# Head outputs stored by ScalarE or from the merge tensor, gates stored by GpSimd, v, q and k split some steps later

## The chip, the cores and the metric

The kernel runs on one core of a Trainium2 chip. A core has engines that work side by side, each through its own instructions in order: TensorE (PE in the profile; PEld is its weight load) multiplies matrices, VectorE (DVE) and ScalarE (ACT) work on elements, GpSimd (POOL) does small work and issues transfers, SyncE (SP) only issues transfers. Transfers (DMA) are issued from the queues of SP, ACT and POOL and are moved by 16 DMA engines. Engines wait for one another by semaphores. The metric is the device time of one execution in microseconds; lower is better.

## The reference

One block of a decoder: 512 rows of width 1024, all in float32. Cut to what matters:

```python
hn = rmsnorm(x, g_mix)
(xa, ba, ca, za, q, k, v, o, zb, ig, fg, ga, gb) = split(hn @ w_in)
ya = (ba * causal_short_conv(ca * xa, conv_w, conv_b) * silu(za)) @ w_a_out
hb = mlstm_chunkwise(q, k, v, ig + b, fg + b)          # 4 heads, dk 256, dv 512
yb = (sigmoid(o) * rmsnorm(hb, g_head) * silu(zb)) @ w_b_out
x  = x + (sigmoid(ga) * ya + sigmoid(gb) * yb) @ w_o
x  = x + sigmoid(rmsnorm(x, g_ple) @ w_ple_gate) * (p @ w_ple)
return rmsnorm(x, g_final)
```

Each head weighs the values v by decayed scores of q and k, divides by a sum, and is normalised and gated.

## The kernel before

**Products.** A float32 operand is split in two: hi, a rounded copy (ACT, L180 for weights), and lo, the rest (DVE, L181). Each product of two operands is three matmuls (L233, L234, L235: hi hi, hi lo, lo hi). Most large products go through `strassen`, which multiplies 2x2 blocks with seven products instead of eight. Product j has two steps of twelve matmuls each (i = 0, 1). Partial results stay in four PSUM banks (acc, bb, cc twice over i); between products ACT takes copies of them (`snap`, L346, tiles s and v) and DVE combines them (`out`, L350) into sums c, of which tag "c" has three buffers. A finished tile goes to a sink: `sink(n, t, src)` gets column half n and row tile t. Products 0 to 6 of a call hand over t2 (n = 0, t = 0 and 1) in steps 4 and 5, t5 and t6 (n = 1) in steps 9 to 13 and the last two tiles (n = 0, t = 2 and 3) straight from PSUM after step 12.

**Weights.** A chunk of weights is loaded by SP (L148) into one of four wraw buffers, split in two halves of 1024 columns, one per step, one product ahead of its use. Sums of chunks that the seven products need are made in place after a split, by an accumulating transfer on POOL's queue (L156, `add_chunk`: it adds a chunk from memory to the tile) or by DVE (L185).

**The order of work.** PE, ACT, DVE and POOL run in the order in which the code is written out. After each step the code calls `step`, and so `tick`: a tick first starts the sinks handed over at the step before, then splits one half of a weight chunk, then takes every running generator (`active`) one `yield` further. A `yield` more is therefore one step later, and what stands at the same tick is queued on each engine in that order. SP's transfers are ordered by the scheduler.

**Tiles.** A pool gives every tag a place (or several); a new tile of a tag waits until all that reads or writes the old one is done. In pool "heads" tag "vv" and tag "qk" have one place each. In turn tag "vv" holds: vv of a head (hi and lo of v), yc (16 KB per partition: blocks to be turned and their result), vv of the next head, and after the last head the tile ya1 of the convolution. Tag "qk" holds qk (hi and lo of q and k), then gty (the gates and the head's output y), then qk of the next head, at last ya0.

**A head** (`head(h, qk)`). A strassen call computes v and o (`sink_vo`): n = 0 tiles are v, split by ACT (L975) and DVE (L978); n = 1 tiles are o, which go through a sigmoid into gty (for odd heads times z, loaded back by POOL at L991). At the same time `scores` runs: score matmuls sc, exponentials on ACT (L916), products on DVE, split into pr. Then come the weighted sums (tile pv) and the normalisation. Even heads have two more strassen calls behind them: z of this head and the next (`sink_z`, stored to z_d by POOL at L1029) and the output gates of the merge (`sink_gate`, L781: a sigmoid, then a store to sg_d from ACT's queue, L782; eight stores a call). Head 2 begins with a call for q and k of heads 2 and 3 (`sink_qk`). The order is: head 0 with z and gates, head 1, head 2 with z and gates, head 3, the convolution (four strassen calls, `sink_conv`), the merge, the last products.

**Turning a head's output** (`turning`, `finish`). y has rows on partitions; the product with w_b_out needs columns there. DVE transposes 32x32 blocks (L810, `turn`), then 16 copies (`move`; ACT at L819, DVE at L817) put the blocks at their places in `spread`, and two transfers (`put`, L822, POOL's queue) store the halves to yt_d, which is loaded again long after. For even heads `finish` runs over the gate call: eight steps of copies, `put(0)`, two turns, six steps of copies, and `put(1)` at the third step of the next head's call. For heads 1 and 3 it runs over the next call and stores both halves at the end.

**q and k of odd heads** (`recut`) were stored to qk_d; during the gate call they are loaded at its eighth step by SP (L869) into a free part of yc and split into qk (L240, L241) three steps later, one of four parts each step.

**The merge tensor** m holds 4 row tiles of 1024 columns. It is allocated after the last head. During the convolution columns 512 and up of row tiles 2 and 3 serve as scratch (ct; L445, L447, L452); the first product of the merge (`gate_conv`, L1155) is the first to write the rest.

Of the kernel before, what the change touches and what calls it, by code (L numbers as in the profile page):

```python
# [20 lines left out]
NH = 4  # L21
# [15 lines left out]
def hybrid_block(ctx, tc, x, p, g_mix, w_in, conv_w, conv_b, w_a_out, b_gates, g_head,  # L37
                 w_b_out, w_o, g_ple, w_ple_gate, w_ple, g_final, out):
    nc = tc.nc
# [30 lines left out]
    H2 = S // 2  # L70
# [197 lines left out]
    yt_d = [dram.tile([P, 2, HC, H2], F32, name=f"yt_d{h}") for h in range(NH)]  # L268
    qk_d = {h: dram.tile([P, 4, S], F32, name=f"qk_d{h}") for h in (1, 3)}
    sg_d = [dram.tile([P, NT, CW], F32, name=f"sg_d{g}") for g in range(4)]  # L270
# [12 lines left out]
    def temp(tag, name=None, dt=F32):  # L283

        return tp.tile([P, S], dt, name=name or tag, tag=tag, bufs={"c": 3}.get(tag, 2))
# [492 lines left out]
    def sink_gate(g):  # L778
        def sink(n, t, src):
            sg = temp("e", "sg") if n == 0 and t > 1 else src  # L780
            act.activation(sg, src, AF.Sigmoid)  # L781
            nc.scalar.dma_start(sg_d[g + n][:, t, :], sg)  # L782
            yield
        return sink

# [10 lines left out]
        a = POFF[j] + (t - j) * P  # L796
        return u[:, a:a + P]

    def turning(h, half):

        both = hp.tile([P, 2, NT, DV], F32, name="yc", tag="vv", align_bytes=256)
        spare, blocks, spread = both[:, 0], both[:, 0], both[:, 1].rearrange("p t v -> p (t v)")
        n = NT
        if half:
            n = NT // 2
            blocks, spread = both[:, 1, :n], both[:, 1, n:].rearrange("p t v -> p (t v)")
        spread = spread.rearrange("p (v s) -> p v s", v=HC)

        def turn(y, t):
            dve.transpose(blocks[:, t % n, :], y[:, t, :])  # L810

        def move(i, on_dve):
            b, q = divmod(i, P // B)
            src = blocks[b * B:(b + 1) * B].rearrange("p t (v q a) -> p t v q a", q=P // B, a=B)[:, :, :, q]
            dst = spread[q * B:(q + 1) * B].rearrange("p v (t b a) -> p t v b a", t=n, a=B)[:, :, :, b]
            if on_dve:
                dve.tensor_copy(dst, src)  # L817
            else:
                act.activation(dst, src, AF.Copy)  # L819

        def put(i):
            nc.gpsimd.dma_start(yt_d[h][:, i], spread if half else spread[:, :, i * H2:(i + 1) * H2])  # L822

        return turn, move, put, spare

    def moves(move, plan):

        todo = deque(range((P // B) ** 2))
        for n_act, n_dve in plan:
            for i in range(max(n_act, n_dve)):  # L830
                if i < n_act:
                    move(todo.popleft(), False)
                if i < n_dve:
                    move(todo.popleft(), True)
            yield
        assert not todo

    def finish(h, y, tools):

        turn, move, put, _ = tools or turning(h, False)  # L840
        if h % 2 == 0:
            yield from moves(move, [(2, 0), (2, 0), (3, 0), (3, 0), (2, 0), (1, 0), (2, 0), (1, 0)])
            put(0)
            for t in (2, 3):
                turn(y, t)
                yield
            yield from moves(move, [(0, 1), (0, 1), (1, 3), (1, 1), (2, 2), (2, 2)])
            put(1)
            return
        for _ in range(4):  # L850
            yield
        for ts in ((0,), (1,), (2,), (3,)) if h == 1 else ((0, 1), (), (2,), (3,)):
            for t in ts:
                turn(y, t)
            yield
        yield from moves(move, [(1, 1)] * 8 if h == 1 else [(3, 0), (3, 1), (2, 1), (1, 1), (2, 2)])
        for i in range(2):
            put(i)

    def qk_tile():  # L860
        both = hp.tile([P, 2, 4, S], F32R, name="qk", tag="qk", align_bytes=256)
# [2 lines left out]
    def recut(h, raw, qk):  # L864

        for _ in range(7):
            yield
        for m in range(4):
            nc.sync.dma_start(raw[:, m, :], qk_d[h][:, m, :])  # L869
        yield  # L870
        yield
        yield
        qk.extend(qk_tile())
        for m in range(4):
            cut(qk[0][:, m, :], qk[1][:, m, :], raw[:, m, :])
            if m < 3:
                yield
# [69 lines left out]
    def head(h, qk):  # L947
        vv = []

        def sink_qk(n, t, src):  # L950

            fs, ps = slice(2 * (t % 2), 2 * (t % 2) + 2), slice(t // 2 * H2, (t // 2 + 1) * H2)
            src = src.rearrange("p (f s) -> p f s", f=2)
            if n == 1:
                nc.gpsimd.dma_start(qk_d[h + 1][:, fs, ps], src)
                return
            for _ in range(4 if t < 2 else 0):
                yield
            if not qk:
                qk.extend(qk_tile())  # L960
            cut(*[u[:, fs, ps] for u in qk], src)
            yield

        if h == 2:
            strassen(hn_lhs, sink_qk, True)
        pr = [hq2.tile([P, 1280], F32R, name=f"pr{i}", align_bytes=256) for i in range(2)]
        pp = hq2.tile([P, 1280], F32, name="pp")
        gt = []

        def sink_vo(n, t, src):  # L970
            if n == 0:
                if not vv:
                    both = hp.tile([P, 2, NT, DV], F32R, name="vv", tag="vv", align_bytes=256)
                    vv.extend(both[:, i] for i in range(2))
                act.activation(vv[0][:, t, :], src, AF.Copy)  # L975
                if t < 2:
                    yield
                dve.tensor_tensor(vv[1][:, t, :], src, vv[0][:, t, :].bitcast(F32), ALU.subtract)  # L978
            elif h % 2:
                so = temp("e", "so")  # L980
                act.activation(so, src, AF.Sigmoid)
                dve.tensor_tensor(gt[0][:, t, :], gt[0][:, t, :], so, ALU.mult)
            else:
                act.activation(gt[0][:, t, :], src, AF.Sigmoid)
            yield

        def scored():
            both = hp.tile([P, 2, NT, DV], F32, name="gty", tag="qk", align_bytes=256)
            gt.extend(both[:, i] for i in range(2))
            if h % 2:  # L990
                nc.gpsimd.dma_start(gt[0], z_d[h])  # L991

        active.append(scores(h, qk, pr, pp, scored))
        strassen(hn_lhs, sink_vo)
        gt, y = gt

        def weighted_sum(t, ps):
            dve.tensor_scalar(y[:, t, :], ps, inv[:, t:t + 1], None, ALU.mult)
            junk = temp("e", "junk")
            act.activation(junk, y[:, t, :], AF.Square, accum_out=hss[:, t:t + 1])  # L1000
            yield

        for t in range(NT):
            ps = ps_x.tile([P, S], F32, name="pv", tag="x")
            for j in range(t + 1):
                mm3(ps, [ptile(u, j, t) for u in pr], [u[:, j, :] for u in vv], j == 0, j == t)
            step(weighted_sum(t, ps))

        def norm(t):
            dve.scalar_tensor_tensor(y[:, t, :], y[:, t, :], hr[:, t:t + 1], gt[:, t, :], ALU.mult, ALU.mult)  # L1010

        def rsqrt():
            a, r, e = htmp
            dve.tensor_scalar(a, hss, 1.0 / DV, EPS, ALU.mult, ALU.add)
            pool.tensor_tensor(r, a, mhalf, ALU.pow)
            yield
            newton(e, a, r)
            dve.tensor_tensor(hr, r, e, ALU.mult)
            for t in range(NT) if h % 2 else ():
                norm(t)  # L1020
                if t == 1:
                    yield

        def sink_z(n, t, src):
            sz = temp("e", "sz")
            act.activation(sz, src, AF.Sigmoid)
            if n == 1:
                dve.tensor_tensor(src, sz, src, ALU.mult)
                nc.gpsimd.dma_start(z_d[h + 1][:, t, :], src)  # L1029
                yield  # L1030
                return
            dve.tensor_tensor(sz, sz, src, ALU.mult)
            dve.tensor_tensor(gt[:, t, :], gt[:, t, :], sz, ALU.mult)
            yield
            norm(t)
            yield
            if t < 2:
                yield
                if not tools:
                    tools.extend(turning(h, True))  # L1040
                tools[0](y, t)
                yield

        tools = []
        active.append(rsqrt())
        if h % 2 == 0:
            strassen(hn_lhs, sink_z)
        return y, tools
# [5 lines left out]
    for h in range(NH):  # L1054
        y, tools = head(h, qks[h])
# [9 lines left out]
    m = mp.tile([P, NT, D], F32, name="m", tag="m")  # L1065
# [216 lines left out]
    half = [slice(0, CW), slice(CW, D)]  # L1282
# [228 lines left out]
```

## Time and profile before

| | us |
|---|---|
| median of 3 runs | 863.88 (863.15 to 866.61) |
| the profiled execution | 864.66 |
| its span, first to last instruction | 862.8 |
| its mean granted TensorE clock | 0.989 |

The span leaves 1.9 us around it. In the profile a row of a group shows the line, engine and operation, out<-in by tile, how often, the busy time and the mean ns of one, and the idle time of the engine just before with what ended it. In the views of waits "A <- B: total, times, longest" says that A stood until B was done. Matmuls overlap, so their time is read from start to start.

### The profile page before, as it was taken

The numbers are of one execution on the slowest core, as the hardware profiler recorded it, in microseconds if no ns is written. First come the engines' busy times: TensorE is split into PE (matmuls) and PEld (weight loads), VectorE is DVE, ScalarE is ACT, GpSimd is POOL, SyncE is SP. The second block draws the span as 40 slices with busy tenths as digits, with TensorE's granted clock in tenths as the row PEclk, the third lists the DMA queues.
The fourth block names the chain that finished last, engine by engine and source line by source line (L and its number), as shares of the span: only waits on it lengthen the run. The fifth ranks groups of instructions, "written<-read, shape, count | busy, mean of one in ns | idle before, by whom it ended". The sixth has DMA issues, their size and how long they took to land.

```text
span 862.8 us, 12094 instructions
## 1 busy us (share of the span) xinstructions
PE 834.4 (97%) x4520; PEld 723.8 (84%) x4520; DVE 672.1 (78%) x927; ACT 528.6 (61%) x783; POOL 213.7 (25%) x207
## 2 busy tenths in 40 slices
PE   9999999999999989999989997999999999999996
PEld 7888888887789968888777996999998888888885
DVE  5787768995688747789758896888885688899665
ACT  6467655876755746667865583555555456567643
POOL 5203131103124411220212334242421122222031
PEclk9999999999999999999999998999999999999998
DMA  9749799679879987995988788898899668999502
GB/s 314 261 135 198 167 219 227 154 244 249 205 163 180 233 210 184 250 214 164 242 211 207 135 197 174 167 185 200 153 232 390 158 167 209 273 268 229 196 1 98
DMA packets 104515, 173.88 MB, mean 202 GB/s; under 512 B 5696, under 2 KB 46196, under 8 KB 103688
## 3 DMA queue, kind: packets, MB, share of 16 engines
q0 software_dynamic: 40064, 70.33, 43.9%
q1 hardware_dynamic: 59792, 94.64, 33.2%
q10 hardware_dynamic: 4600, 8.14, 3.1%
q8 instruction: 35, 0.57, 0.3%
q14 instruction: 24, 0.20, 0.1%
HBM read 156.30 MB, written 16.79 MB: 201 GB/s over the span
## 4 chain that ended last, share of the span: by engine, by line
PE 79%; DMA 6%; ACT 6%; DVE 4%; issue 3%; POOL 1%; ACTq 0%; SPq 0%; POOLq 0%; DVEq 0%
PE mm L235 24%; PE mm L234 24%; PE mm L233 24%; DMA yt_d<-yc 5%; ACT whi L180 2%; DVE wlo L181 2%; PE pv L234 1%; PE pv L233 1%; PE pv L235 1%; DMA gty<-z_d 1%; ACT yc L819 1%; DMA xin<-in_x 1%; POOL wraw L156 1%; ACT qk L240 1%; ACT c L781 0%
## 5 line engine op out<-in xcount | busy, mean ns | idle before, releaser
L181 DVE TENSOR_TENSOR wlo<-wraw,whi 128x1024 fp32r<-128x1024 f32 x244 | 299.2, 1227 | 109.2 <-ACT whi L180 103.5
L180 ACT ACTIVATE whi<-wraw 128x1024 fp32r<-128x1024 f32 x246 | 257.9, 1054 | 87.1 <-PE mm L235 34.4
L156 POOL DMA_DIRECT2D wraw<-in_w_in x112 | 137.5, 1410 | 342.3 <-DVE wlo L181 277.8
L233 PE MATMUL mm<-whi,hs 128*128 128x512 f32 x256 | 101.2, 395 | 8.2 <-ACT v L346 8.2
L234 PE MATMUL mm<-wlo,hs 128*128 128x512 f32 x256 | 101.2, 395 | 0.3 <-DVE wlo L181 0.3
L235 PE MATMUL mm<-whi,hs 128*128 128x512 f32 x256 | 101.1, 395 | 0.0
L346 ACT ACTIVATE s<-mm 128x512 f32<-128x512 f32 x84 | 50.2, 598 | 82.0 <-PE mm L235 80.5
L235 PE MATMUL mm<-hn_hi,wlo 128*128 128x256 f32 (+1 forms) x304 | 93.9, 309 | 6.5 <-DVE wlo L181 6.4
L233 PE MATMUL mm<-hn_hi,whi 128*128 128x256 f32 (+1 forms) x304 | 93.9, 309 | 0.0
L234 PE MATMUL mm<-hn_lo,whi 128*128 128x256 f32 (+1 forms) x304 | 93.4, 307 | 0.0
L235 PE MATMUL mm<-hs,wlo 128*128 128x256 f32 x320 | 90.6, 283 | 0.0
L233 PE MATMUL mm<-hs,whi 128*128 128x256 f32 x320 | 90.6, 283 | 0.0
L234 PE MATMUL mm<-hs,whi 128*128 128x256 f32 x320 | 90.6, 283 | 0.0
L234 PE MATMUL mm<-wlo,hn_hi 128*128 128x512 f32 x192 | 75.5, 393 | 3.6 <-DVE wlo L181 3.6
L233 PE MATMUL mm<-whi,hn_hi 128*128 128x512 f32 x192 | 74.9, 390 | 0.0
L235 PE MATMUL mm<-whi,hn_lo 128*128 128x512 f32 x192 | 74.8, 390 | 0.0
L235 PEld LDWEIGHTS mm<-hn_hi,wlo 128*128 128x128 f32 x304 | 58.7, 193 | 9.7 <-DVE wlo L181 6.9
L233 PEld LDWEIGHTS mm<-whi,hs 128*128 128x128 f32 x256 | 48.7, 190 | 18.7 <-ACT v L346 8.8
L234 PEld LDWEIGHTS mm<-hs,whi 128*128 128x128 f32 x320 | 61.5, 192 | 0.0
L233 PEld LDWEIGHTS mm<-hs,whi 128*128 128x128 f32 x320 | 61.5, 192 | 0.0
L235 PEld LDWEIGHTS mm<-hs,wlo 128*128 128x128 f32 x320 | 61.5, 192 | 0.0
L233 PEld LDWEIGHTS mm<-hn_hi,whi 128*128 128x128 f32 x304 | 58.8, 193 | 2.4
(340 smaller groups left out, 1726.3 us busy)
## 6 DMA issues: line engine op xcount, KB each, us to landing
wraw<-in_w_in SPq DMA_DIRECT2D x32, 1024.0 KB, 5.3
wraw<-in_w_in POOLq DMA_DIRECT2D x52, 512.0 KB, 7.9
wraw<-in_w_in SPq DMA_DIRECT2D x48, 512.0 KB, 4.9
wraw<-in_w_in POOLq DMA_DIRECT2D x60, 256.0 KB, 5.8
wraw<-in_w_b_out SPq DMA_DIRECT2D x7, 1024.0 KB, 6.4
wraw<-in_w_b_out POOLq DMA_DIRECT2D x12, 512.0 KB, 6.5
wraw<-in_w_o SPq DMA_DIRECT2D x5, 1024.0 KB, 7.9
yt_d<-yc POOLq DMA_DIRECT2D x8, 512.0 KB, 8.8
```

The lines of the kernel that those rows point to most:

```text
L156: nc.gpsimd.dma_start(raws[to][:, ks, cs], src[:, ks, :], accum_op=ALU.add)
L180: act.activation(hi, t, AF.Copy)
L181: (e_lo or dve).tensor_tensor(lo, t, hi.bitcast(F32), ALU.subtract)
L233: pe.matmul(ps, lhsT=a[0], rhs=b[0], start=first, stop=False, **kw)
L234: pe.matmul(ps, lhsT=a[0], rhs=b[1], start=False, stop=False, **kw)
L235: pe.matmul(ps, lhsT=a[1], rhs=b[0], start=False, stop=last, **kw)
L240: act.activation(hi, src, AF.Copy)
L346: act.activation(to[i], src, AF.Copy, scale=scale)
L819: act.activation(dst, src, AF.Copy)
```

## The change

1. The gates of the merge are stored from GpSimd's queue (sixteen stores).
2. The second half of the turned outputs of heads 0 and 2, and both halves of head 1, are stored from ScalarE's queue; the first half of heads 0 and 2 and both of head 3 stay with GpSimd.
3. For the last six steps of copies of even heads the plan (copies by ACT, by DVE) is another; ACT makes 4 instead of 6 and DVE 12 instead of 10.
4. The last head's copies put the blocks into row tiles 0 and 1 of m instead of the second half of yc, and the stores read m.
5. q and k of odd heads are split 2 steps later after their load.
6. In heads 1 to 3 the first two row tiles of v are split 4 steps later.

```diff
 def sink(n, t, src):
     sg = temp("e", "sg") if n == 0 and t > 1 else src
     act.activation(sg, src, AF.Sigmoid)
-    nc.scalar.dma_start(sg_d[g + n][:, t, :], sg)
+    nc.gpsimd.dma_start(sg_d[g + n][:, t, :], sg)
     yield
...
-def turning(h, half):
+def turning(h, half, place=None):
...
+    if place is not None:
+        spread = place.rearrange("p t v -> p (t v)")
     spread = spread.rearrange("p (v s) -> p v s", v=HC)
...
-    def put(i):
-        nc.gpsimd.dma_start(yt_d[h][:, i], spread if half else spread[:, :, i * H2:(i + 1) * H2])
+    def put(i, queue=nc.gpsimd):
+        queue.dma_start(yt_d[h][:, i], spread if half else spread[:, :, i * H2:(i + 1) * H2])
...
 def finish(h, y, tools):
-    turn, move, put, _ = tools or turning(h, False)
+    turn, move, put, _ = tools or turning(h, False, m[:, :2, :] if h == NH - 1 else None)
     if h % 2 == 0:
...
-        yield from moves(move, [(0, 1), (0, 1), (1, 3), (1, 1), (2, 2), (2, 2)])
-        put(1)
+        yield from moves(move, [(1, 2), (1, 2), (0, 2), (0, 2), (1, 2), (1, 2)])
+        put(1, nc.scalar)
         return
...
     for i in range(2):
-        put(i)
+        put(i, nc.scalar if h == 1 else nc.gpsimd)
...
 def recut(h, raw, qk):
...
-    yield
-    yield
-    yield
+    for _ in range(5):
+        yield
     qk.extend(qk_tile())
...
 def sink_vo(n, t, src):
     if n == 0:
+        for _ in range(4 if t < 2 and h else 0):
+            yield
         if not vv:
```

## What the change is predicted to do

> **What bounds the kernel now.** First the page: the span and the engines' busy time.
>
> ```profile
> span 862.8 us, 12094 instructions
> ...
> PE 834.4 (97%) x4520; PEld 723.8 (84%) x4520; DVE 672.1 (78%) x927; ACT 528.6 (61%) x783; POOL 213.7 (25%) x207
> ```
>
> TensorE (PE) is the bound at 97% busy. The change removes no matmul, so it can only close PE's idle time. The view of waits, for PE alone, names who ended that (total, times, longest):
>
> ```profile
> PE mm L233 <- ACT v L346: 8.2, 3, 3.9
> PE mm L235 <- DVE wlo L181: 6.4, 1, 6.4
> PE mm L234 <- DVE wlo L181: 3.9, 6, 0.9
> ```
>
> That is 18.5 us. The chain of waits (start, us, what) shows what stood behind the first two rows:
>
> ```profile
> 207.06 10.13 DMA yt_d<-yc
> 217.38 0.44 issue
> 217.81 0.59 ACT v L346
> 218.44 0.50 PE mm L233
> ...
> 300.47 11.76 DMA yt_d<-yc
> ...
> 433.46 10.15 DMA yt_d<-yc
> ...
> 520.03 7.52 DMA yt_d<-yc
> 527.57 0.69 DVE ya L410
> ```
>
> All four are one pattern. The store of a head's turned outputs still reads `yc`; the next tile of tag `vv` (vv at L975, ya at L410) has the same place; the in-order engine that first writes it stands, and behind it the splits and snapshots that PE needs. The gaps sum to 8.2 + 6.4 = 14.6 us: the three in the heads, the longest 3.9, and one in the convolution. The third, from PE's waits between 444 and 470 us, is
>
> ```profile
> PE mm L233 <- ACT v L346: 2.2, 1, 2.2
> ```
>
> so the first is 8.2 - 3.9 - 2.2 = 2.1 us. A gap can also cost clock afterwards. In the view by stretches of time the granted clock is the third number from the end of a row:
>
> ```profile
> 217.00:232.00 15.00, 13.55 (x55) 11.15 (x56) 10.98 (x17) 10.14 (x18) 3.01 (x3) 0.89 0.78 161
> ...
> 444.00:460.00 16.00, 14.82 (x67) 12.06 (x68) 13.03 (x20) 12.25 (x20) 2.99 (x3) 1.00 0.78 189
> ```
>
> ```profile
> 314.00:316.00 2.00, 2.00 (x7) 1.25 (x7) 1.57 (x2) 2.00 (x6) 0.00 (x0) 0.66 0.01 2
> 316.00:318.00 2.00, 2.00 (x5) 1.53 (x5) 1.24 (x3) 2.00 (x5) 0.00 (x0) 0.50 0.57 140
> ...
> 530.00:532.00 2.00, 1.95 (x9) 1.95 (x10) 1.93 (x4) 0.00 (x0) 0.00 (x0) 0.50 0.34 79
> 532.00:534.00 2.00, 2.00 (x15) 2.00 (x14) 1.93 (x5) 0.00 (x0) 1.26 (x2) 0.73 1.06 373
> ```
>
> Time lost is length times (1 - clock): 15 x 0.11 = 1.65 after the first gap, 0.68 + 1.00 after the second, nothing after the third, 1.00 + 0.54 after the fourth; 4.9 us. The four gaps are worth 14.6 + 4.9 = **19.5 us**: 11.6 in the heads (8.2 + 3.3), 7.9 in the convolution (6.4 + 1.5).
>
> [...]
>
> **The change part by part.** A step of the seven-product routine is twelve matmuls:
>
> ```profile
> 226.33 0.39 PE L233 MATMUL mm<-whi,hs 128*128 128x512 f32 x1
> ...
> 229.05 0.39 PE L233 MATMUL mm<-whi,hs 128*128 128x512 f32 x1
> ```
>
> That is 2.72 us; score matmuls lengthen some steps.
>
> *v split 4 steps later (heads 1 to 3).* The vv write leaves the queue in front of snapshot L346 and comes 4 x 2.72 = 10.9 us later. The longest hold was 3.9 us, so this part alone should clear the head gaps: **11.6 us**. It moves, per head, two ACT splits and two DVE subtractions; the weighted sums that need them stand at the end of the call, three steps or more behind. The sums c that they read are held longer: of the three buffers of c, each is rewritten one step after its late subtraction, by DVE itself, so DVE's own order covers it. One step less and DVE would stand for 2.7 us.
>
> *Turned outputs stored by ScalarE (second half of heads 0 and 2, both halves of head 1).* Four issues leave POOL's queue, where they stood among accumulating loads, for ACT's. With the 10.9 us above no one waits for their landing, so sooner landing is costed at nothing; without that cover it would be worth up to the gaps. What an issue costs ACT (timeline of ACT):
>
> ```profile
> 189.58 0.33 ACTq L782 DMA_DIRECT2D sg_d<-c  x1
> 189.96 0.60 ACT L346 ACTIVATE s<-mm 128x512 f32<-128x512 f32 x1 [0.41 <-ACT c L781]
> ```
>
> That is 0.41 us. The issue now also waits on ACT for DVE's last copies, and behind it stand that step's exponentials and snapshots. Two in a row are 0.8 us, hidden by an ACT that is 61% busy; uncovered they cost that 0.8 us.
>
> *Gates stored by GpSimd.* Sixteen issues leave ACT, 16 x 0.41 = 6.6 us of it, mostly in the stretches just before heads 1 and 3, where PE waits for late splits (waits of PE between 180 and 206 us):
>
> ```profile
> PE mm L234 <- DVE wlo L181: 1.2, 2, 0.8
> ```
>
> With six of eight issues gone there (2.5 us of ACT) these 1.2 us should go too, and as much at the second gate call, which has the same code: I take **2.4**; bounds 0 and the third row's 3.9. On POOL the nearest row is the store of z, same size from the same buffers by the same queue; here its landing, and DVE's wait for it to free c:
>
> ```profile
> DMA to landing us min/median/max: 2.7/6.5/8.1
> ```
>
> ```profile
> DVE c L350 <- DMA z_d<-c: 0.7, 2, 0.4
> ```
>
> So 0.4 us of DVE per call from early stores; at 8.1 us a store would hold c about 5 us longer, and DVE with it. Each store also stands before the next accumulating load on POOL. Both ends go into the allowance below.
>
> *Copies and q, k.* Heads 0 and 2 turn two more blocks on DVE and two fewer on ACT in as many steps; the four q, k cuts come two steps later, still two steps ahead of the score matmuls. With one cut a step on each engine this evens out: nothing; were that distance gone, PE would wait up to a step, 2.7 us.
>
> *Head 3's outputs in the merge tensor.* The store reads m, so ya waits only for the copies, which end before it. The next writes of m (L445, L447) go to other tiles and columns of it. DVE then need not stand from 520.03 to 527.57, and the split that ended the fourth gap is ready some 7.5 us earlier, before PE needs it: **7.9 us**.
>
> *What is late next.* In odd heads z's load; the waits of DVE:
>
> ```profile
> DVE gty L982 <- DMA gty<-z_d: 2.9, 2, 2.0
> ```
>
> The late v subtractions fall into this wait, which hides them; they would else push the splits by up to 1.4 us per head. Then the accumulating loads: in the stretch from 204 to 218 us they land late,
>
> ```profile
> wraw<-in_w_in POOLq DMA_DIRECT2D x2, 512.0 KB, 10.6
> ```
>
> and today's gaps hide that. A chunk is split again four steps after its addition, 10.9 us, of which the split and the subtraction ahead of the issue take 1.1 + 1.2 = 2.3 us; PE needs it one product (5.4 us) later, less another 2.3:
>
> ```profile
> L181 DVE TENSOR_TENSOR wlo<-wraw,whi 128x1024 fp32r<-128x1024 f32 x244 | 299.2, 1227 | 109.2 <-ACT whi L180 103.5
> L180 ACT ACTIVATE whi<-wraw 128x1024 fp32r<-128x1024 f32 x246 | 257.9, 1054 | 87.1 <-PE mm L235 34.4
> ```
>
> So PE waits only if a load takes over some 10.9 - 2.3 + 5.4 - 2.3 = 11.7 us. At 10.6 it is close. For all this I allow **2.0 us** (bounds 0 and 9).
>
> Sum: 19.5 + 2.4 - 2.0 = 19.9 us. The span 862.8 becomes 842.9, and with the 1.9 us around it (the profiled run took 864.66) 844.8. The median of the runs, 863.88, lies 0.8 below that run, which gives 844.0. I predict **844.0 us**; its own range is 839.5 (no allowance, all small waits of the third row gone, 1 us of spread) to 847 (allowance 5).
>
> **The rivals.**
>
> *Late loads eat part.* Stores of gates on POOL and no gaps to hide behind: two or three loads late by 2 to 3 us, 4 to 9 us in all, 847 to 852. For it: 10.6 against 11.7. Against: the turned outputs leave that queue. [...]
>
> *m is held whole.* If writes of m wait for the store, the convolution's 7.9 us stay: 851.9. Against, from the code alone: other parts of m are written, turned and read apart throughout.
>
> *The change doesn't do what it says in the heads.* vv still waits, for another reader of its place: 11.6 us stay, 855.6; with the convolution also, 863.5.
>
> *Slower.* One mechanism: accumulating loads beyond 11.7 us in every head. The view of line L156 gives their landing:
>
> ```profile
> DMA to landing us min/median/max: 4.4/6.1/15.5
> ```
>
> At the longest, 15.5, PE stands 3.8 us and loses some 1.7 of clock, 5.5 per operand; at four the gain is spent, at six (two for each of three heads) 844.0 + 33 = 877. Against: the median is 6.1.
>
> **How the numbers follow.** Forecast 0.66, late loads 0.15, m held 0.06, heads unchanged or nothing at all 0.08, slower 0.05. A measurement of this kernel tells about 0.5%, 4.3 us, from no change. The range 839.5 to 852 takes in the first three, 0.87. Faster by over 0.5% (below 859.6) holds these and part of the fourth: 0.89; within, 0.06; slower 0.05.
>
> **What would show it.** Right: no PE wait on L346 and none over 1 us on L181; no wait of L975 or L410 for yt_d; clock 1.00 throughout the heads; gates issued on POOL with no stall of L350 over 0.5 us. Wrong: splits (L180) waiting for accumulating loads with PE behind them, L445 or L447 waiting for yt_d, or ACT standing at an issue of yt_d.

## The result, and the profile after

The kernel before took 864.55 us (median of 4 runs, 863.15 to 866.61), the changed one 845.06 us (4 runs, 843.33 to 846.08). The ratio is 0.9771, 95% interval 0.9744 to 0.9797: faster by 19.8 us by the ratio (19.5 between the medians), where 19.9 were forecast. The profiled execution took 846.08 us.

Code behind the edits has moved down a little: the turned outputs are now stored at L824, `sink_vo` splits v at L978 and L981, z is loaded at L994. L180, L181, L346, L350, L410 and L782 are where they were.

The page of the changed kernel, first its span and busy times, then the granted clock in 40 slices:

```profile
span 844.0 us, 12126 instructions
...
PE 829.3 (98%) x4520; PEld 720.5 (85%) x4520; DVE 673.2 (80%) x931; ACT 526.0 (62%) x779; POOL 219.6 (26%) x219
...
PEclk9999999999999999999999999999999999999999
```

The two pages already divide the gain. PE's idle time (span less busy) was 862.8 - 834.4 = 28.4 us and is 844.0 - 829.3 = 14.7: 13.7 us of the 18.8 that the span lost. The other 5.1 us are PE's own busy time; the lower clock after the gaps had stretched it by 4.9 in the prediction's count.

To see where the idle time was, take the view by stretches of 50 us. A row gives the stretch, its length, PE's busy time with its matmuls, the granted clock, the DMA share and GB/s. Before:

```profile
200.00:250.00 50.00, 47.10 (x207) 0.97 0.91 215
...
300.00:350.00 50.00, 46.09 (x203) 0.97 0.84 202
...
400.00:450.00 50.00, 46.02 (x206) 1.00 0.89 236
450.00:500.00 50.00, 49.13 (x311) 1.00 0.81 183
500.00:550.00 50.00, 43.48 (x349) 0.93 0.81 172
```

After:

```profile
200.00:250.00 50.00, 49.40 (x243) 1.00 0.97 228
...
300.00:350.00 50.00, 49.07 (x222) 1.00 0.94 226
...
400.00:450.00 50.00, 48.48 (x218) 1.00 0.97 248
450.00:500.00 50.00, 48.78 (x354) 1.00 0.78 166
500.00:550.00 50.00, 49.87 (x416) 1.00 0.93 203
```

The lengths less the busy times add up to 18.2 us before and 4.4 after. In the convolution (last row) almost nothing is left and the clock is whole. In the heads some 4.3 us remain. The waits of PE, all of them, say who ends these:

```profile
PE mm L234 <- DVE wlo L181: 3.2, 4, 1.2
PE mm L491 <- DVE hn_lo L486: 1.5, 1, 1.5
PE mm L233 <- ACT whi L180: 0.9, 2, 0.8
PE pt L550 <- DVE xin L545: 0.5, 1, 0.5
PE mm L233 <- DVE c L350: 0.2, 1, 0.2
```

L346 is gone, and so is the 6.4 us at L235. (L491 and L550 belong to the beginning of the kernel.) What is left are splits of weights, L180 and L181, 4.1 us. Their last ones, in the timeline of PE between 440 and 456 us (start, duration, instruction; in brackets the idle time ahead of it and who ended it):

```profile
440.29 0.51 PE L233 MATMUL mm<-whi,hs 128*128 128x512 f32 x1 [0.75 <-ACT whi L180]
...
441.55 0.51 PE L234 MATMUL mm<-wlo,hs 128*128 128x512 f32 x1 [0.76 <-DVE wlo L181]
...
453.92 0.50 PE L234 MATMUL mm<-wlo,hn_hi 128*128 128x512 f32 x1 [1.22 <-DVE wlo L181]
```

And the chain of waits of the changed kernel that leads to them (start, us, what):

```profile
412.57 23.12 DMA wraw<-in_w_in x2
...
435.71 1.07 ACT whi L180
...
436.81 1.24 DVE wlo L181
...
442.52 8.82 DMA gty<-z_d
...
452.04 0.68 DVE c L350
452.73 1.15 DVE wlo L181
...
453.92 0.50 PE mm L234
```

Two accumulating loads, 23.12 us together, come in late; ACT stands for the second and splits at 435.71. The wait at 453.92 has z's load, 8.82 us, ahead of it. ACT's waits for weights show the same pressure over the whole kernel. Before:

```profile
ACT whi L180 <- DMA wraw<-in_w_in: 8.8, 12, 1.6
```

After:

```profile
ACT whi L180 <- DMA wraw<-in_w_in: 29.0, 19, 4.1
```

So the pattern that was predicted as next is what now stands there: stores no longer hold PE, loads do, in smaller pieces.

### The profile page after: what moved, and what is told of

Same layout as the page of the kernel before. It is cut to its first block, busy times and chain, and to the rows that moved or that the text cites. A ratio compares the mean times of both kernels' runs of the same rounds, so it can differ in the third digit from the quotient of the medians.

```text
span 844.0 us, 12126 instructions
## 1 busy us (share of the span) xinstructions
PE 829.3 (98%) x4520; PEld 720.5 (85%) x4520; DVE 673.2 (80%) x931; ACT 526.0 (62%) x779; POOL 219.6 (26%) x219
## 4 chain that ended last, share of the span: by engine, by line
PE 72%; DMA 10%; issue 9%; DVE 4%; ACT 3%; POOL 2%; SPq 0%; POOLq 0%; DVEq 0%; ACTq 0%
PE mm L234 22%; PE mm L235 22%; PE mm L233 22%; DMA wraw<-in_w_in 8%; DVE wlo L181 2%; ACT whi L180 1%; PE pv L234 1%; PE pv L233 1%; PE pv L235 1%; DMA gty<-z_d 1%; DMA xin<-in_x 1%; POOL sg_d L782 1%; POOL wraw L156 0%; PE ptk L1307 0%; PE pth L1188 0%
## 5 line engine op out<-in xcount | busy, mean ns | idle before, releaser
L181 DVE TENSOR_TENSOR wlo<-wraw,whi 128x1024 fp32r<-128x1024 f32 x244 | 299.5, 1228 | 98.6 <-ACT whi L180 92.8
L180 ACT ACTIVATE whi<-wraw 128x1024 fp32r<-128x1024 f32 x246 | 257.8, 1054 | 96.6 <-PE mm L235 34.2
L233 PE MATMUL mm<-whi,hs 128*128 128x512 f32 x256 | 100.2, 391 | 1.1 <-ACT whi L180 0.9
L235 PE MATMUL mm<-whi,hs 128*128 128x512 f32 x256 | 99.8, 390 | 0.0
L346 ACT ACTIVATE s<-mm 128x512 f32<-128x512 f32 x84 | 50.1, 597 | 76.3 <-PE mm L235 75.1
L235 PE MATMUL mm<-hn_hi,wlo 128*128 128x256 f32 (+1 forms) x304 | 93.3, 307 | 0.1
L235 PE MATMUL mm<-hs,wlo 128*128 128x256 f32 x320 | 90.8, 284 | 0.0
L235 PE MATMUL mm<-whi,hn_lo 128*128 128x512 f32 x192 | 74.8, 390 | 0.0
L235 PEld LDWEIGHTS mm<-hs,wlo 128*128 128x128 f32 x320 | 61.5, 192 | 0.0
L235 PEld LDWEIGHTS mm<-hn_hi,wlo 128*128 128x128 f32 x304 | 58.1, 191 | 3.2 <-DVE wlo L181 0.3
L234 PEld LDWEIGHTS mm<-hn_lo,whi 128*128 128x128 f32 x304 | 58.2, 191 | 2.4
```

The lines of the kernel that those rows point to most:

```text
L180: act.activation(hi, t, AF.Copy)
L181: (e_lo or dve).tensor_tensor(lo, t, hi.bitcast(F32), ALU.subtract)
L233: pe.matmul(ps, lhsT=a[0], rhs=b[0], start=first, stop=False, **kw)
L234: pe.matmul(ps, lhsT=a[0], rhs=b[1], start=False, stop=False, **kw)
L235: pe.matmul(ps, lhsT=a[1], rhs=b[0], start=False, stop=last, **kw)
L346: act.activation(to[i], src, AF.Copy, scale=scale)
```

## The experiments

The theory was that of the prediction: the delay of v frees the heads, the place in m frees the convolution, and what is left are late accumulating loads. The first rival gave the credit in the heads to the queues (sooner landing of the turned outputs). Later ones asked what the small edits are worth. Ratios are to the kernel before on the same chip.

| kernel | median us (range) | ratio (95%) |
|---|---|---|
| changed, v not delayed | 854.95 (853.94 to 855.20) | 0.9878 (0.9864 to 0.9891) |
| changed, all turned outputs stored by GpSimd | 848.75 (846.85 to 852.38) | 0.9813 (0.9792 to 0.9835) |
| changed, head 3 turned in yc | 856.36 (854.34 to 857.14) | 0.9893 (0.9879 to 0.9906) |
| changed, gates stored by ScalarE | 844.80 (843.01 to 848.70) | 0.9758 (0.9745 to 0.9771) |
| changed, once more | 845.29 (843.12 to 849.35) | 0.9782 (0.9758 to 0.9806) |
| changed, old gates, copies and q, k steps | 845.53 (844.62 to 846.80) | 0.9779 (0.9763 to 0.9796) |
| changed, one addition of four by DVE | 839.17 (838.67 to 840.64) | 0.9710 (0.9693 to 0.9726) |
| the same with gates stored by ScalarE | 840.35 (839.69 to 841.17) | 0.9712 (0.9693 to 0.9731) |
| before, v delayed | 854.39 (853.11 to 854.56) | 0.9878 (0.9861 to 0.9894) |
| before, v delayed and the place in m | 846.51 (845.80 to 847.91) | 0.9786 (0.9766 to 0.9806) |
| the same with one addition by DVE | 842.50 (842.22 to 842.67) | 0.9736 (0.9718 to 0.9755) |

### The delay of v, taken away and alone

```diff
 def sink_vo(n, t, src):
     if n == 0:
-        for _ in range(4 if t < 2 and h else 0):
-            yield
```

> The changed kernel with the v split at once again, as before; all else of the change stays. Theory of the prediction (the four steps alone clear the head gaps): the 11.6 us of the heads come back at least in part, 851 to 857 us, with ACT standing at vv (L975 of before) for yt_d before heads 1, 2 and 3. Rival (the earlier issue and landing on ScalarE's queue suffice): in the changed kernel the store of head 0 is issued at 201.74 us and lands 8.3 us later, before the split of v would come in the old place at some 210 us, so heads 1 and 3 stay clear and only head 2, whose two stores together were the longest hold, gives something back: 844 to 849 us.

854.95 us: by the ratios 0.0096 to 0.0107 of 865 us, 8.3 to 9.3 us, come back. Yet the waits of PE, in the heads, name one gap and not three:

```profile
PE mm L233 <- ACT v L346: 7.7, 1, 7.7
```

It is head 2's, after both halves of head 1's outputs went to ScalarE's queue. Its chain:

```profile
293.74 19.25 DMA yt_d<-yc
...
313.07 0.10 ACT vv L976
...
314.24 0.79 PE mm L233
```

In heads 1 and 3 the stores land in time even without the delay. So the amount is the theory's and the manner is half the rival's: without the delay the other edits clear two gaps and lengthen the third from 3.9 to 7.7 us, and the clock is at 0.50 from 313 to 319 us. ScalarE's queue is the simplest reason (head 0's second store is issued at 202.7 us and lands 8.9 us later; in the kernel before at 207.1 us, and 10.1 us later), but the queue by itself was not run. Taking the delay out of the changed kernel therefore doesn't measure its worth in the kernel before. Adding it there does:

```diff
 def sink_vo(n, t, src):
     if n == 0:
+        for _ in range(4 if t < 2 and h else 0):
+            yield
```

> The kernel before with nothing but the v split four steps later in heads 1 to 3. Theory of the prediction: the three head gaps go whole, 11.6 us, less some 2 to 3 us of late loads as in the changed kernel: 853 to 857 us, no wait of PE on the snapshot L346, the convolution's gap of 6.4 us as before. Rival (without the other edits the next thing in the heads is as late): 859 us or more.

854.39 us, a gain of 10.1, with all stores still on GpSimd's queue. L346 is gone from the waits of PE, the convolution's gap stays:

```profile
PE mm L235 <- DVE wlo L181: 6.2, 1, 6.2
PE mm L234 <- DVE wlo L181: 3.4, 6, 0.8
```

The delay by itself clears all three gaps of the heads.

### The place in the merge tensor

```diff
-    turn, move, put, _ = tools or turning(h, False, m[:, :2, :] if h == NH - 1 else None)
+    turn, move, put, _ = tools or turning(h, False, None)
```

> The changed kernel with the last head's outputs turned inside yc again, stored from there by GpSimd. Theory: the convolution's gap comes back in full, 7.9 us with its clock: 852 to 854 us, with DVE at L410 of before waiting for yt_d and PE idle some 6 us after it. Rival (ACT and DVE come there earlier now and the store lands before it is waited for): under 848 us.

856.36 us, above the 852 to 854 expected: by the ratios 0.0111 to 0.0122 of 865 us, 9.6 to 10.6 us, come back. The chain of this kernel has the old gap:

```profile
510.96 7.02 DMA yt_d<-yc
...
518.08 0.69 DVE ya L410
...
520.56 0.58 PE mm L235
```

PE's wait there is 6.0 us, and the clock is lower behind it (stretch, length, busy times of the five engines, clock, DMA share, GB/s):

```profile
520.00:525.00 5.00, 4.44 (x21) 4.45 (x22) 4.72 (x10) 0.00 (x0) 1.76 (x2) 0.50 0.66 209
```

From 520.56 to 525 at half clock are 2.2 us; 6.0 + 2.2 = 8.2. The rest of the 10 us is in small waits in the heads (6.6 us in this profiled execution, 4.1 in that of the changed kernel); why they are longer here was not traced. The same place in m, put into the kernel before together with the delay of v and nothing else:

> The kernel before with only two edits: v split four steps later, and the last head's outputs turned into the merge tensor. Theory (these two carry the whole gain; queues, copies and q, k are worth nothing): only_delay measured 854.4 us, less the convolution's 7.9 gives 846.5 us; 844.5 to 847.5 us. Rival (the other edits carry part of it): 848.5 us or more.

846.51 us, ratio 0.9786 against 0.9878: 8.0 us. These two edits together give 18.5 us (0.0214 of 865) of the 19.8; the intervals of this kernel and the changed one, 0.9766 to 0.9806 and 0.9744 to 0.9797, overlap.

### The queues

```diff
-            put(1, nc.scalar)
+            put(1)
...
-        put(i, nc.scalar if h == 1 else nc.gpsimd)
+        put(i)
```

> The changed kernel with all turned outputs stored by GpSimd again; v is still split four steps later. Theory (the four steps clear the gaps whatever the queue): 844 to 847 us, no wait for yt_d; a small loss since the stores stand among the accumulating loads again. Rival (the queue did it): the head gaps come back, 851 to 857 us.

848.75 us, some 3 us more than the changed kernel and above the 844 to 847 expected; the intervals overlap a little. Nothing waits for yt_d. What is longer are the waits for splits:

```profile
PE mm L234 <- DVE wlo L181: 3.8, 5, 1.0
PE mm L233 <- ACT whi L180: 2.7, 3, 2.0
```

That is 6.5 us against 4.1. With gates and turned outputs both on GpSimd's queue, stores stand in front of the accumulating loads there. That this order is the whole of the 3 us was not tried apart.

```diff
-            nc.gpsimd.dma_start(sg_d[g + n][:, t, :], sg)
+            nc.scalar.dma_start(sg_d[g + n][:, t, :], sg)
```

> The changed kernel with the gates stored from ScalarE's queue again. Theory of the prediction (ACT is relieved by 0.41 us for each of 16 stores): 2.4 us are given back, 846 to 849 us, with PE waiting for wlo before heads 1 and 3. Rival (the stores now stand before the accumulating loads on GpSimd's queue, and the changed kernel's remaining 4 us of PE waits come from such late loads): ACT's waits for wraw fall well below the 29.0 us of the changed kernel and the time is the same or lower, 841 to 845 us.

> The changed kernel itself once more, as the measure for the runs beside it: 843 to 847 us, ratio 0.974 to 0.980 as at first.

844.80 us with the gates back on ScalarE, 845.29 for the changed kernel once more. By the ratios the gates on ScalarE are even 1.1 to 2.1 us faster, with intervals that overlap: the move of the gates is worth nothing that these runs can tell. The rival's sign is no clearer: ACT's waits for wraw, 24.1 us, lie between the 23.8 and 29.0 of the changed kernel's two profiles.

### The copies and the q, k steps

```diff
-            nc.gpsimd.dma_start(sg_d[g + n][:, t, :], sg)
+            nc.scalar.dma_start(sg_d[g + n][:, t, :], sg)
...
-            yield from moves(move, [(1, 2), (1, 2), (0, 2), (0, 2), (1, 2), (1, 2)])
+            yield from moves(move, [(0, 1), (0, 1), (1, 3), (1, 1), (2, 2), (2, 2)])
...
-        for _ in range(5):
+        for _ in range(3):
             yield
```

> The changed kernel with gates on ScalarE's queue (as in gates_act, 844.8 us) and besides q and k split after three steps and the copies planned as before. Theory A (the moved q, k cuts and copies, not the queue of the gates, took away the small waits of PE for wlo before heads 1 and 3, 1.2 and 1.5 us in the kernel before): those waits come back, 2 to 4 us over gates_act, 846.5 to 849 us. Theory B (they went because the head gaps and the ACT backlog behind them went): no such waits, within 1 us of gates_act.

845.53 us, the same again, but the waits have moved. PE's waits between 180 and 225 us, ahead of and in head 1, in this kernel:

```profile
PE mm L234 <- DVE wlo L181: 1.2, 2, 0.8
```

and between 395 and 440 us, ahead of head 3:

```profile
PE mm L234 <- DVE wlo L181: 1.5, 2, 0.8
```

These 2.7 us are just what the kernel before has there. The changed kernel has none of them, and with only the gates put back they are 0.3 and 0.5 us. So the waits are theory A's and the time is theory B's. Taken off in this order, the copies and the q, k steps remove 1.9 us and the gates the last 0.8.

ACT's timeline between 190 and 199 us shows why the parts can't be priced one by one. There a step of ACT, from one split L180 to the next, takes 4.05 and 4.09 us in this kernel, 3.49 and 3.51 with the copies and q, k steps of the change, and 2.65 and 2.72 with the gates moved as well, which is PE's own step of 2.72. All of it stands in one in-order queue, and PE waits only for what is too much.

Why the whole returned nothing is seen in PE's waits for splits in the heads: they are 2.2 us in this kernel, 3.5 with only the gates put back, 4.1 and 3.0 in the two profiles of the changed kernel. With those ahead of heads 1 and 3 the sums are 4.9, 4.2, 4.1 and 3.0 us, too near to one another for runs that spread over 2 to 6 us. ACT's waits for weights go the same way (19.6, 24.1, 29.0 and 23.8 us). That PE comes sooner to loads that are not there yet is the reading that fits; the next runs try it.

### The loads themselves

If late accumulating loads are what is left, fewer of them must remove it. Four sums of chunks are needed for each half of a head's call; in the changed kernel all are accumulating transfers. Here one of the four is made by DVE (L185) in heads 1 to 3, from a chunk that is loaded anyway, two products later. This takes six transfers of 512 KB off GpSimd's queue:

```diff
     for h in range(NH):
-        pair(w_in_v, [(V + h * DV, DV)], [(O + h * DV, DV)])
+        pair(w_in_v, [(V + h * DV, DV)], [(O + h * DV, DV)], 1 if h else 0)
```

> The changed kernel with one of the four additions of weight chunks of the v and o call (heads 1 to 3) made by DVE instead of an accumulating load: 1 MB less through the DMA engines per head, 2.4 us more of DVE. Theory (the 4 us of PE waits that remain come from accumulating loads that land late among saturated DMA engines): ACT's waits for wraw fall from 29.0 to under 20 us, PE's waits in the heads to under 2 us, 841.5 to 844 us. Rival (DVE is the tight engine of the heads): PE waits more for wlo, 846 us or more.

839.17 us, 6 us below the changed kernel and the fastest of all; the theory had expected no less than 841.5. ACT's waits for wraw are 14.1 us. The waits of PE are these two, both at the beginning of the kernel:

```profile
PE mm L491 <- DVE hn_lo L486: 1.5, 1, 1.5
PE pt L550 <- DVE xin L545: 0.7, 1, 0.7
```

And two stretches of 20 us, head 3's, where the changed kernel stood; the columns are those of the row at 520 us above. Changed:

```profile
420.00:440.00 20.00, 19.52 (x92) 15.86 (x90) 9.19 (x12) 11.06 (x20) 3.58 (x3) 1.00 1.01 252
440.00:460.00 20.00, 17.74 (x76) 14.17 (x77) 18.25 (x36) 14.60 (x22) 2.80 (x4) 1.00 0.80 212
```

With the addition by DVE:

```profile
420.00:440.00 20.00, 20.00 (x97) 16.91 (x96) 15.90 (x21) 14.54 (x27) 4.21 (x4) 1.00 0.94 222
440.00:460.00 20.00, 20.00 (x98) 16.89 (x97) 17.68 (x34) 13.36 (x23) 4.90 (x4) 1.00 0.76 187
```

The DMA share falls from 1.01 to 0.94 and from 0.80 to 0.76, and PE is busy throughout. DVE has 6.3 us more to do in the whole kernel (673.2 to 679.5 busy) and the time for it; most of the step from 9.19 to 15.90 us in the first stretch is work that no longer waits for loads. Of the 6.9 us between the two spans (844.0 and 837.1), PE's idle time makes 4.1; the other 2.8 are spread over its busy time and weren't traced further. Against the second profile of the changed kernel (span 841.1) the two parts are 2.8 and 1.2. The addition by DVE also comes two products later than the transfer did; that was not tried apart.

Two more kernels ask what the small edits are worth once the loads are in time. With the gates on ScalarE again:

> dve_add with the gates stored from ScalarE's queue again. Theory (the queue of the gates is worth nothing): within 1 us of dve_add's 839.2 us. Rival of the prediction (ACT is relieved by the move, 2.4 us): 841 us or more, with PE waiting for wlo before heads 1 and 3.

840.35 us, ratio 0.9712 against 0.9710: still nothing clear of the spread, though 0.9 us of PE's waits for wlo are back before heads 1 and 3. And the addition by DVE on top of the two large edits alone, without any of the small ones:

> The two edits, and one addition of weight chunks per v and o call of heads 1 to 3 on DVE, as in dve_add (839.2 us). Theory (with fewer accumulating loads the queue of the stores does not matter): 838.5 to 841 us. Rival (the stores on GpSimd's queue still stand before the loads that remain): 842 us or more, with PE waiting for late splits in the heads.

842.50 us, ratio 0.9736, which is 2.2 us above 0.9710 (the intervals overlap slightly). Beside the 840.35 of the run before, on the same chip and with the gates on ScalarE in both, it is 2.15 us, and the ranges lie apart. So it is the rival's time, and the waits of PE have the small ones back:

```profile
PE mm L234 <- DVE wlo L181: 2.5, 4, 0.8
```

They stand ahead of heads 1 and 3, as in the kernel before, so they are those of the splits rather than of late loads (ACT's waits for wraw are 8.2 us). So the copies, the q, k steps and the queue of the turned outputs are worth some 2 us together where the loads don't take it back. Which of them carries how much of that wasn't run.

## Why the prediction was right, and where it was not

**The four gaps, 19.5 us: right.** They closed, all four, by the two edits that were named. The convolution's 7.9 measured 8.0. The heads' 11.6 measured 10.1 between the medians of the delay alone, and 11.5 between the spans of the two profiled executions (862.8 and 851.3); the runs beside it of the kernel before go from 862.95 to 867.41. Late loads don't explain a shortfall: PE's waits for splits are 3.9 us in both profiles, though ACT's waits for weights have gone from 8.8 to 17.6 us. For idle time and clock 14.6 and 4.9 were predicted; PE's idle and busy time fell by 13.7 and 5.1 us in the first profile of the changed kernel and by 15.0 and 6.7 in the second, so the division holds to some 2 us.

**Longest hold 3.9 us, delay 10.9 us: right, but the hold was read at PE.** What the delay has to cover is ACT's stand at vv. ACT's waits have it as 8.3 us at the longest in the kernel before, and as 11.5 us in head 2 of the kernel with the stores on ScalarE and no delay; PE felt 3.9 and 7.7 of them. Four steps cover the first whole and the second all but 0.6, and nothing waited. Fewer steps weren't run.

**The clock's price: the sum read from the trace holds to some 2 us (4.9 predicted, 5.1 and 6.7 found), its size for one gap does not carry over.** The gap in the convolution cost 1.5 us of clock in the kernel before and 2.2 in the kernel that has it back; 6.4 and 6.0 us of idle time. Behind the gaps of 6.0 and 7.7 us the clock was 0.50. In the kernel before it was 0.89 over the 15 us behind the gap of 2.1 us, which lost 1.65, and 1.00 around the gap of 2.2 us, which lost nothing: the length of a gap alone does not tell its price here.

**Gates stored by GpSimd, 2.4 us: the step that failed.** Its place was right, its cause was half of it. The waits before heads 1 and 3, 1.2 and 1.5 us, did go; but the gates took only the last 0.8 of the 2.7. The other 1.9 went by the copies and the q, k steps, which the prediction had costed at nothing: ACT's step there fell from 4.1 to 3.5 us by them and from 3.5 to 2.7 by the gates. Which of copies and q, k steps did it is open. In time the gates alone are worth nothing that was measured: 844.80 against 845.29 us, and 0.9712 against 0.9710.

**The allowance of 2.0 us for late loads: right in kind, and in PE's waits near the size.** Of the third row's 3.9 us in the kernel before, 2.7 lay ahead of heads 1 and 3 and 1.2 in the heads; in the changed kernel 4.1 lie in the heads, in its second profile 3.0. That is 2.9 or 1.8 us more, where 2.0 were allowed. Yet easing the loads gained 6 us in time, and of that only the part in PE's waits is accounted for. Of small terms 2.4 - 2.0 = 0.4 was predicted; 2.7 - 2.9 = -0.2 or 2.7 - 1.8 = 0.9 was found. That the gain was met to 0.1 us by the ratio is luck: 844.0 and the median of 845.06 are 1.1 apart, and the runs of the changed kernel spread over 6 us.

**z's load hides the late v subtractions: right**, but no more than that. DVE's wait for gty was 2.9 us in two heads, is 0.5 with the delay alone and 1.1 in the changed kernel, where the wait of 1.22 us at PE stands behind it.

**Sooner landing is worth nothing: right as argued, for a reason that was half missed.** With the delay nobody waits for yt_d, on either queue. But the queue also decides what stands before the accumulating loads, and the some 3 us of the kernel with all turned outputs on GpSimd may be that; it was not tried apart. The prediction had this as a mark in favour of the change, without a price.

**The rivals.** m is not held whole: no wait of L445 or L447 for yt_d. The delay did what it says. The time stayed below the 847 to 852 of the late loads, but their mechanism was at work. Of the signs of being wrong one is there, splits (L180) that wait for accumulating loads with PE behind them, and one wait on L181 is over 1 us (1.22). The 6 us that easing the loads gained lie within that rival's 4 to 9.

The slower case had its condition and not its price. Loads beyond 11.7 us did come in all three heads, but in the changed kernel PE lost at most 1.5 us behind those of one head, not 3.8 for each load: the threshold was too low. In the DMA view of the changed kernel, the accumulating loads issued between 203 and 209 us and those issued between 420 and 426 us (number, KB, median us to landing):

```profile
wraw<-in_w_in POOLq DMA_DIRECT2D x2, 512.0 KB, 13.0
...
wraw<-in_w_in POOLq DMA_DIRECT2D x2, 512.0 KB, 14.5
```

The first two took 12.9 and 13.2 us: ACT stood for them, PE didn't. Behind the other two, 14.9 and 14.0 us, PE stood 0.75 and 0.76 us, at 440 to 442. One term of the working explains 1.2 us: it takes 2.3 us for both halves of a split before PE starts, but in the rows at 440.29 and 441.55 PE starts with hi and needs lo 1.26 us later. The rest is open. Nor was 10.6 us the number to hold against a threshold: it is a median, and in the kernel before single loads issued at 208, 301 and 434 us already took 11.8, 13.4 and 12.2 us.

## What to carry to other kernels

When an in-order engine stands at the first write of a tile whose place is still being stored, writing later, or storing from somewhere else, closed every gap here, worth 10.1 us in the heads (11.6 predicted) and 8.0 in the convolution (7.9); with the other edits alone, the store's queue among them, two gaps closed and the third grew from 3.9 to 7.7 us. A closed gap brings the next work forward by its length, so look for what had its lead time from that gap, here the accumulating loads (ACT's waits for weights went from 8.8 to 29.0 us), and lighten it in the same change. A small wait that an edit removed was worth nothing so long as the engine then waited as long for something later (2.7 us of waits gone, 845.29 against 845.53 us): judge small edits with the later wait taken away, and together where they fill the same queue. Hold a threshold against single transfers, not against their median (here 11.8 to 13.4 us beside a median of 10.6).

## What was not expected of the hardware

Stores from ScalarE's queue landed later than the same stores from GpSimd's in one place (17.0 us against 11.8) and sooner in another (8.3 against 13.4). Both halves of head 1's outputs, issued between 290 and 297 us, in the DMA view of the changed kernel (two queues, q0 GpSimd's and q10, with packets, MB and share of the 16 engines; then the issues):

```profile
q0 software_dynamic: 621, 1.31, 94.2%
...
q10 hardware_dynamic: 76, 0.08, 3.1%
...
yt_d<-yc ACTq DMA_DIRECT2D x2, 512.0 KB, 17.0
```

and in the kernel before with v delayed:

```profile
yt_d<-yc POOLq DMA_DIRECT2D x2, 512.0 KB, 11.8
```

17.0 us against 11.8, in a stretch in which GpSimd's queue (q0) with its accumulating loads holds 94% of the engines' time. In the changed kernel with all turned outputs on GpSimd's queue it is 13.1. For the one store of head 0 that was moved it is the other way round, in the DMA views from 200 to 206 us of the changed kernel and of the one with all turned outputs on GpSimd's queue:

```profile
yt_d<-yc ACTq DMA_DIRECT2D x1, 512.0 KB, 8.3
...
yt_d<-yc POOLq DMA_DIRECT2D x1, 512.0 KB, 13.4
```

Head 2's is alike, 7.8 against 13.5 us. Head 1 has two such stores one behind the other; whether that makes the difference was not tried. Between 290 and 297 us q10 moved 76 packets, q0 621. The stores were issued between 291 and 294 us; what else was waiting then is not in the trace, so why they land late stays open.
